# A hybrid encoder layer on one core: the last two and the first two input-projection tiles of adjacent blocks run in pairs

## The chip, the cores and the metric

The kernel runs on 1 core of one Trainium2 chip. The metric is device time in microseconds (us) of one execution. The time before is the median of three runs.

## What is computed

One layer, 2048 tokens, width 1024, all in float32:

```python
h = rms_norm(x, norm1_g)
p = h @ w_in                       # one projection, columns split among four mixers
o = concat([fox_attention(p_A), gated_delta(p_B), hgrn2(p_C), gla(p_D)])
x = x + o @ w_out
x = x + conv_glu_ffn(rms_norm(x, norm2_g))
```

The change is about `p = h @ w_in` alone: which of its column tiles run when.

## The kernel before

The tokens are cut into four blocks of 512. For each block `in_proj(b)` computes the projection in 23 tiles of 128 columns (`proj_fm`) and three of 256 (`proj_tm`). A float32 product is made of three matmuls on a high and a low part of each operand (`mm3`: L108 high by high, L109 high weights by low `h`, L110 low weights by high `h`), so that a 128-column tile over the eight row groups k of `h` takes 24 matmuls. Below, such a matmul with 512 columns of `h` is called a big one. `h` of a block lies in sixteen tiles `h_hi0..7` and `h_lo0..7`, one buffer each: `block_h(b)` loads each piece of x from HBM (L295, into a `w2` tile of a ring of five), multiplies it by the row scale on VectorE (L296), and writes `h_hi` on ScalarE (L300) and `h_lo` on VectorE (L301). So `h_hi[k]` of block b+1 can be written only after the last tile of block b has read `h_hi[k]`.

Weights come in halves of four k (`load_half`: a load into one of two `w_raw` tiles, L315, then a split into `w_hi`, L306 on ScalarE, and `w_lo`, L307 on VectorE, four buffers each). A tile's result lies in one of three PSUM banks `ps_mm` and leaves it through ScalarE; for a gate tile `put` runs a SiLU in five steps (L119 to L123, ScalarE and VectorE in turn), and stores the result to `p_scr` (L373). The SiLU's two buffers come from the same `w2` ring as x.

The tiles of a block come in this order: the gates' tile `FM_SMALL`, six tiles of the delta-rule mixer from `FM_GQ` on, HGRN2 and GLA tiles, and at last the gates of three mixers, between which the FoX tiles (`group_fox`, its last part the 256-column tile `TM_FV` with stores to `v_scr`, L893) are spread. The last three of a block before: `FM_LG, TM_FV, FM_LG + 1`; then block b+1 begins with `block_h`, `FM_SMALL` (`small_gates`, L412 on, a chain over ScalarE and VectorE that ends in a scan, L425, and eight transposes on TensorE, L436), and `FM_GQ`.

The projection is one stream of Python steps; the three linear mixers (`group_gdn`, `group_hg`, `group_gla`) are three others, and `weave` traces the step of whichever stream is due first: each step says how long it counts (`yield 0.25`). Work under `self.first()` gets a higher priority. The framework's scheduler then puts every engine's instructions into one fixed order, by these priorities and by when it reckons operands and buffers to be ready; each engine works its order off without overtaking, and so does SyncE's queue of DMAs. Small matmuls of the mixers (L647 to L670 the delta rule, L732 to L739 the attention pieces of HGRN2 and GLA) so stand between the big ones. After block 3's last tile the projection's pools close, and FoX attention loads its heads (L964).

Of the kernel before, what the change touches and what calls it, by code (L numbers as in the profile page):

```python
# [10 lines left out]
F32 = mybir.dt.float32  # L11
# [10 lines left out]
KT = D // 128  # L22
# [3 lines left out]
TB = 512  # L26
# [11 lines left out]
FM_SMALL, FM_FQ, FM_FK, FM_GQ, FM_GK, FM_GV, FM_GZ = 0, 1, 3, 5, 7, 9, 11  # L38
FM_HQ, FM_HF, FM_HG, FM_LQ, FM_LK, FM_LG = 13, 15, 17, 19, 20, 21
N_FM = 23  # L40
P_G, P_HF, P_HQ, P_LQ, P_LK, P_GATE, N_P = 0, 6, 8, 10, 11, 12, 18
# [37 lines left out]
class Kernel:  # L79
# [245 lines left out]
    def proj_fm(self, t):  # L325
# [5 lines left out]
                yield 0.25  # L331
        return ps

    def proj_tm(self, t, consume):
        mm = self.nc.tensor.matmul
        ps = [self.ps_mm.tile([128, 2, 256], F32, name="ps_mm") for _ in range(2)]
        for kk in range(4):
            hi, lo = self.load_half(self.i["w_tm"][t, kk])
            for tt in range(4):
                o = ps[tt // 2][:, tt % 2]  # L340
                ts = slice(tt * 128, (tt + 1) * 128)
                for k in (2 * kk, 2 * kk + 1):
                    s = slice(k % 2 * 256, k % 2 * 256 + 256)
                    mm(o, self.h_hi[k][:, ts], hi[:, s], start=(k == 0 and tt % 2 == 0), stop=False,  # L344
                       skip_group_check=True)
                    mm(o, self.h_hi[k][:, ts], lo[:, s], start=False, stop=False, skip_group_check=True)  # L346
                    mm(o, self.h_lo[k][:, ts], hi[:, s], start=False, stop=(k == KT - 1), skip_group_check=True)  # L347
                if tt % 2 and 2 * kk + tt // 2 < 6:
                    yield 0.125
        for tt in range(4):  # L350
            consume(tt, ps[tt // 2][:, tt % 2])

    def in_proj(self, b):
        nc = self.nc
        bs = slice(b * TB, (b + 1) * TB)
        with self.first():
            self.block_h(b, self.first_block() if b == 0 else None)
            for _ in self.small_gates(b):
                pass
        stats = self.block_stats(b + 1) if b < NB - 1 else iter(())  # L360
        def put(t, slot, scale=None, gate=None):
            next(stats, None)
            ps = yield from self.proj_fm(t)
            with self.first():
                o = self.w2()
                if gate is not None:
                    tmp = self.w2()
                    self.silu(o, ps, tmp, gate)
                elif scale is not None:
                    nc.scalar.activation(out=o, in_=ps, func=AF.Copy, scale=scale)  # L370
                else:
                    nc.scalar.copy(out=o, in_=ps)
                nc.sync.dma_start(out=self.p_scr[slot, :, bs], in_=o)  # L373
        def put_v(t, w):
# [3 lines left out]
                    nc.scalar.copy(out=o, in_=ps)  # L378
                    nc.sync.dma_start(out=self.lv_scr[w, b, :, tt], in_=o)
            yield from self.proj_tm(t, consume)  # L380
        yield
        for j in range(6):
            yield from put(FM_GQ + j, P_G + j)
            yield 0.25
        for j in range(2):
# [14 lines left out]
        for n, (t, c) in enumerate(((FM_GZ, C_GON), (FM_HG, C_HON), (FM_LG, C_LON))):  # L400
            for j in range(2):
                if n + j:
                    for size in fox:
                        yield size or 0.25
                        if not size:
                            break
                yield from put(t + j, P_GATE + 2 * n + j, gate=self.col(c))
                yield 0.25
        assert next(fox, self) is self


    def small_gates(self, b):  # L412
        nc = self.nc
        ps = yield from self.proj_fm(FM_SMALL)
        z = self.wg()
        nc.scalar.activation(out=z, in_=ps, func=AF.Identity, scale=self.col(C_SIGN), bias=self.sbias)
        nc.sync.dma_start(out=self.gk_scr[b], in_=z[0:16, :])
# [1 line left out]
        w = self.wg()  # L419
# [13 lines left out]
        for w, (t, r) in enumerate(((G, 96), (ls, 64))):  # L433
            ps = self.ps.tile([128, TB], F32, name="ps")
# [1206 lines left out]
```

## Time and profile before

| | us |
|---|---|
| median of three runs | 2995.86 (2993.44 to 3003.88) |
| the profiled execution | 2996.68 |
| its span, first to last instruction | 2994.9 |
| TensorE busy in the span | 2864.3 (96%) |
| VectorE busy | 2152.0 (72%) |
| ScalarE busy | 1596.3 (53%) |
| mean granted TensorE clock | 0.967 |

The page of a profile lists busy times, the chain of work that ended last and the costliest groups of instructions. The trace behind it answers finer questions: an engine's instructions in order of time, with the idle time before each and what ended it; busy time and granted clock by stretch. Times count from the span's first instruction. A clock of 1.00 is 2.4 GHz, of 0.50 is 1.2 GHz.

### The profile page before, as it was taken

How to read it: one execution, taken by the hardware profiler on the slowest of the kernel's cores; microseconds unless marked ns; L12 is line 12 of the kernel's file. 1: busy time of each engine (PE TensorE's matmuls, PEld its weight loads, DVE VectorE, ACT ScalarE, POOL GpSimd, SP SyncE). 2: the span in 40 equal slices, each digit the busy share in tenths (PEclk: the TensorE clock that was granted, in tenths of full speed). 3: DMA queues.
4: the chain of work that ended last, by engine and by line, in shares of the span. 5: the costliest groups of instructions: out<-in, count | busy, mean ns of one | idle time of the engine just before them, and what ended most of it. 6: DMA issues, size and time to landing. Idle time of an engine off the chain costs nothing.

```text
span 2994.9 us, 57398 instructions
## 1 busy us (share of the span) xinstructions
PE 2864.3 (96%) x21994; PEld 2335.9 (78%) x21994; DVE 2152.0 (72%) x4666; ACT 1596.3 (53%) x3171; POOL 127.5 (4%) x258
## 2 busy tenths in 40 slices
PE   7999999999999998999999999999999999999999
PEld 5777777787777777777788888878788888888787
DVE  6697778678767876667666655558777777886975
ACT  6575667566656665555666632343455544544443
POOL 0000010001000100000000000003000000000000
PEclk9999999799889997999999999999999999999999
DMA  5633463355235523876533322453222221847344
GB/s 179 183 100 126 139 181 100 112 165 166 80 104 171 165 66 103 222 205 203 137 107 103 102 67 66 141 184 116 85 84 75 85 85 60 281 142 242 130 136 145
DMA packets 268938, 400.08 MB, mean 134 GB/s; under 512 B 66612, under 2 KB 93124, under 8 KB 268152
## 3 DMA queue, kind: packets, MB, share of 16 engines
q1 hardware_dynamic: 268664, 396.43, 43.5%
q8 instruction: 172, 2.82, 0.4%
q14 instruction: 102, 0.84, 0.1%
HBM read 310.63 MB, written 85.70 MB: 132 GB/s over the span
## 4 chain that ended last, share of the span: by engine, by line
PE 73%; DVE 9%; DMA 9%; ACT 6%; issue 2%; SPq 0%; DVEq 0%; ACTq 0%
PE ps_mm L108 15%; PE ps_mm L109 15%; PE ps_mm L110 14%; PE pt L108 3%; PE pt L110 3%; PE pt L109 3%; DVE w_lo L307 2%; PE po L1033 2%; DMA w_raw<-w_fm 2%; PE pt L1019 2%; PE ps L732 1%; ACT w_hi L306 1%; PE ps_mm L344 1%; PE ps_mm L346 1%; PE ps_mm L347 1%
## 5 line engine op out<-in xcount | busy, mean ns | idle before, releaser
L307 DVE TENSOR_TENSOR w_lo<-w_raw,w_hi 128x512 fp32r<-128x512 f32 x386 | 268.8, 698 | 199.7 <-ACT w_hi L306 188.1
L306 ACT CAST w_hi<-w_raw 128x512 fp32r<-128x512 f32 x386 | 237.7, 617 | 281.2 <-PE ps_mm L109 179.4
L108 PE MATMUL ps_mm<-h_hi,w_hi 128*128 128x512 f32 x736 | 314.8, 429 | 15.7 <-ACT h_hi L300 7.7
L108 PE MATMUL ps_mm<-h,w_hi 128*128 128x512 f32 x768 | 308.2, 402 | 2.6 <-ACT h L1208 1.7
L109 PE MATMUL ps_mm<-h,w_hi 128*128 128x512 f32 x768 | 303.9, 396 | 0.0
L109 PE MATMUL ps_mm<-h_lo,w_hi 128*128 128x512 f32 x736 | 303.5, 413 | 0.0
L110 PE MATMUL ps_mm<-h,w_lo 128*128 128x512 f32 x768 | 303.4, 396 | 0.0
L110 PE MATMUL ps_mm<-h_hi,w_lo 128*128 128x512 f32 x736 | 302.1, 411 | 0.5 <-issue 0.4
L108 PE MATMUL ps_mm<-big,w_hi 128*128 128x512 f32 x456 | 183.6, 404 | 11.1 <-ACT big L306 6.7
L108 PEld LDWEIGHTS ps_mm<-h_hi,w_hi 128*128 128x128 f32 x736 | 144.3, 197 | 54.8 <-ACT h_hi L300 10.5
L110 PE MATMUL ps_mm<-big,w_lo 128*128 128x512 f32 x456 | 181.8, 399 | 0.0
L109 PE MATMUL ps_mm<-big,w_hi 128*128 128x512 f32 x456 | 181.7, 399 | 0.0
L110 PEld LDWEIGHTS ps_mm<-h,w_lo 128*128 128x128 f32 x768 | 144.4, 188 | 33.8
L108 PEld LDWEIGHTS ps_mm<-h,w_hi 128*128 128x128 f32 x768 | 144.1, 188 | 33.1 <-ACT h L1208 2.7
L110 PEld LDWEIGHTS ps_mm<-h_hi,w_lo 128*128 128x128 f32 x736 | 144.6, 196 | 31.0 <-DVE w_lo L307 1.5
L109 PEld LDWEIGHTS ps_mm<-h,w_hi 128*128 128x128 f32 x768 | 144.6, 188 | 30.9 <-DVE h L1209 1.4
L109 PEld LDWEIGHTS ps_mm<-h_lo,w_hi 128*128 128x128 f32 x736 | 144.6, 196 | 30.7 <-issue 3.2
L306 ACT CAST w_hi<-fo 128x512 fp32r<-128x512 f32 x135 | 79.5, 620 | 104.4 <-issue 36.8
L1238 DVE SCALAR_TENSOR_TENSOR y<-u,fconv,y 128x512 f32<-128x512 f32 x176 | 131.8, 749 | 3.8
L1382 DVE SCALAR_TENSOR_TENSOR y<-u,fconv,y 128x1024 f32<-128x1024 f32 x88 | 112.8, 1282 | 19.5 <-ACT y L1380 18.7
L307 DVE TENSOR_TENSOR p_lo<-pt,p_hi 128x512 fp32r<-128x512 f32 (+1 forms) x144 | 93.9, 657 | 37.9 <-ACT p_hi L306 37.8
L108 PE MATMUL pt<-w_hi 128*128 128x512 f32 x308 | 120.3, 391 | 0.0
(414 smaller groups left out, 7306.4 us busy)
## 6 DMA issues: line engine op xcount, KB each, us to landing
w_raw<-w_fm SPq DMA_DIRECT2D x184, 256.0 KB, 3.1
w_raw<-w_up SPq DMA_DIRECT2D x88, 256.0 KB, 2.6
fo<-w_down SPq DMA_DIRECT2D x88, 256.0 KB, 3.5
fo<-a_scr SPq DMA_DIRECT2D x88, 256.0 KB, 4.4
wr<-w_up SPq DMA_DIRECT2D x84, 256.0 KB, 2.7
p_scr<-w SPq DMA_DIRECT2D x72, 256.0 KB, 2.7
w_raw<-w_out SPq DMA_DIRECT2D x64, 256.0 KB, 3.7
w_raw<-w_tm SPq DMA_DIRECT2D x48, 256.0 KB, 3.0
```

The costliest lines, as they stand in the source:

```text
L108: mm(ps, w_hi, x_hi, start=start, stop=False, **k)
L109: mm(ps, w_hi, x_lo, start=False, stop=False, **k)
L110: mm(ps, w_lo, x_hi, start=False, stop=stop, **k)
L306: self.nc.scalar.copy(out=hi, in_=src)
L307: self.nc.vector.tensor_tensor(out=lo, in0=src, in1=f32(hi), op=ALU.subtract)
L344: mm(o, self.h_hi[k][:, ts], hi[:, s], start=(k == 0 and tt % 2 == 0), stop=False, skip_group_check=True)
L346: mm(o, self.h_hi[k][:, ts], lo[:, s], start=False, stop=False, skip_group_check=True)
L347: mm(o, self.h_lo[k][:, ts], hi[:, s], start=False, stop=(k == KT - 1), skip_group_check=True)
L1019: nc.tensor.transpose(pt[:, x * 128:x * 128 + 128], P[t][:, kt * 128:kt * 128 + 128], self.ident)
L1033: mm(po[:, c0:c0 + cn], vst[:, kt], part[:, kk * 256:kk * 256 + cn], start=(kt == 0 and part is hi), stop=(kt == nkt - 1 and part is lo), ...
L1238: nc.vector.scalar_tensor_tensor(out=y, in0=u[:, i:i + TB], scalar=w(i), in1=y, op0=ALU.mult, op1=ALU.add)
L1382: nc.vector.scalar_tensor_tensor(out=yt, in0=u[g][:, i:i + 2 * TB], scalar=f(i), in1=yt, op0=ALU.mult, op1=ALU.add)
```

## The change

`proj_pair` computes two tiles in step: for each k, six matmuls, three for either tile, and then a yield. `FM_SMALL` and `FM_GQ` are one pair, `FM_LG` and `FM_LG + 1` the other. The first pair is no longer under `first()` and traced at one go: it gives 0.25 of a step after each k, so that the mixers' steps are traced between. `TM_FV` now comes before both `FM_LG` tiles instead of between them. The two results of a pair are taken (`take`) after both are complete. `small_gates` gets its tile ready made.

```diff
+    def proj_pair(self, *ts):
+
+        out = [self.ps_mm.tile([128, TB], F32, name="ps_mm") for _ in ts]
+        for k in range(KT):
+            if k % 4 == 0:
+                w = [self.load_half(self.i["w_fm"][t][:, k // 4 * TB:(k // 4 + 1) * TB]) for t in ts]
+            s = slice(k % 4 * 128, k % 4 * 128 + 128)
+            for o, (hi, lo) in zip(out, w):
+                self.mm3(o, hi[:, s], lo[:, s], self.h_hi[k], self.h_lo[k], k == 0, k == KT - 1)
+            if k < KT - 1:
+                yield 0.25
+        return out
+
...
             self.block_h(b, self.first_block() if b == 0 else None)
-            for _ in self.small_gates(b):
-                pass
+        ps, gq = yield from self.proj_pair(FM_SMALL, FM_GQ)
+        with self.first():
+            self.small_gates(b, ps)
...
-        yield
-        for j in range(6):
+        take(gq, P_G)
+        yield 0.25
+        for j in range(1, 6):
...
-                yield from put(t + j, P_GATE + 2 * n + j, gate=self.col(c))
-                yield 0.25
+                if n < 2:
+                    yield from put(t + j, P_GATE + 2 * n + j, gate=self.col(c))
+                    yield 0.25
+        for j, ps in enumerate((yield from self.proj_pair(t, t + 1))):
+            take(ps, P_GATE + 4 + j, gate=self.col(c))
+        yield 0.25
```

The number of instructions on each engine stays as it was; their order changes, on TensorE from the first block to the start of the output projection, and not behind it. Lines below L334 stand 13 to 20 higher in the new kernel (L654 becomes L674).

On TensorE, the end of block 0 in the kernel before (`h_hi_240` and `h_hi_245` are k = 6 and 7, `h_lo_241` and `h_lo_246` their low parts; `ps_3477` a PSUM tile of a mixer):

```order
L108 MATMUL ps_mm<-h_hi_240,w_hi 128x512
L109 MATMUL ps_mm<-h_lo_241,w_hi 128x512
L110 MATMUL ps_mm<-h_hi_240,w_lo 128x512
L108 MATMUL ps_mm<-h_hi_245,w_hi 128x512
L109 MATMUL ps_mm<-h_lo_246,w_hi 128x512
L110 MATMUL ps_mm<-h_hi_245,w_lo 128x512
L782 MATMUL psl<-wl,l_kT 128x128 x2
L654 MATMUL ps<-g_R,w_2409 64x64 x4
L732 MATMUL ps_3477<-wl 32x32 x4
```

The same place now:

```order
L108 MATMUL ps_mm<-h_hi_245,w_hi 128x512
L109 MATMUL ps_mm<-h_lo_246,w_hi 128x512
L110 MATMUL ps_mm<-h_hi_245,w_lo 128x512
L108 MATMUL ps_mm<-h_hi_245,w_hi 128x512
L109 MATMUL ps_mm<-h_lo_246,w_hi 128x512
L110 MATMUL ps_mm<-h_hi_245,w_lo 128x512
L802 MATMUL psl<-wl,l_kT 128x128 x2
L674 MATMUL ps<-g_R,w_2409 64x64 x4
L752 MATMUL ps_3434<-wl 32x32 x4
L752 MATMUL ps_3434<-wx 32x32 x13
L682 MATMUL ps<-g_vn,w_1249 64x64 x4
```

Six big matmuls now use one k where three did, and from here to the first big matmul of block 1 stand 142 small matmuls (of the delta rule 8 `g_R`, 16 `g_vn`, 2 `gS`) where 124 stood (4, 4 and none).

The first big matmuls of block 1 before (`h_hi_3341` is k = 0, `h_hi_3348` k = 1, `h_hi_3355` k = 2):

```order
L108 MATMUL ps_mm<-h_hi_3341,w_hi 128x512 x2
L109 MATMUL ps_mm<-h_lo_3342,w_hi 128x512
L110 MATMUL ps_mm<-h_hi_3341,w_lo 128x512
L108 MATMUL ps_mm<-h_hi_3348,w_hi 128x512
L109 MATMUL ps_mm<-h_lo_3349,w_hi 128x512
L110 MATMUL ps_mm<-h_hi_3348,w_lo 128x512
L109 MATMUL ps_mm<-h_lo_3342,w_hi 128x512
L110 MATMUL ps_mm<-h_hi_3341,w_lo 128x512
```

and now:

```order
L108 MATMUL ps_mm<-h_hi_3341,w_hi 128x512 x2
L752 MATMUL ps_3645<-wl 32x32
L109 MATMUL ps_mm<-h_lo_3342,w_hi 128x512
L110 MATMUL ps_mm<-h_hi_3341,w_lo 128x512
L109 MATMUL ps_mm<-h_lo_3342,w_hi 128x512
L110 MATMUL ps_mm<-h_hi_3341,w_lo 128x512
L108 MATMUL ps_mm<-h_hi_3348,w_hi 128x512
L109 MATMUL ps_mm<-h_lo_3349,w_hi 128x512
```

Both tiles were already begun together; the second one's k = 0 now ends before k = 1 begins.

On SyncE's queue at the same boundary before (`w_raw<-x` belongs to the row scale of the block after; `w_raw<-w_fm` are weights; `w_3316` is the SiLU's result of `FM_LG + 1`):

```order
L252 DMA w_raw<-x 128x512
L315 DMA w_raw<-w_fm 128x512 x2
L295 DMA w_3338<-xT 128x512
L295 DMA w_3345<-xT 128x512
L373 DMA p_scr<-w_3316 128x512
L295 DMA w_3352<-xT 128x512
L295 DMA w_3359<-xT 128x512
```

and now (`w_3308` is the SiLU's result of `FM_LG`):

```order
L252 DMA w_raw<-x 128x512
L315 DMA w_raw<-w_fm 128x512
L389 DMA p_scr<-w_3308 128x512
L315 DMA w_raw<-w_fm 128x512
L295 DMA w_3338<-xT 128x512
L295 DMA w_3345<-xT 128x512
L389 DMA p_scr<-w_3316 128x512
L295 DMA w_3352<-xT 128x512
L295 DMA w_3359<-xT 128x512
```

The store of a SiLU's result now stands ahead of the first load of x.

## Rows read from the trace of the kernel before

**Rows 1.** The page, part 4: the chain that ended last, by engine.
```profile
PE 73%; DVE 9%; DMA 9%; ACT 6%; issue 2%; SPq 0%; DVEq 0%; ACTq 0%
```
**Rows 2.** Busy by stretch: length, PE, PEld, DVE, ACT, POOL, clock, DMA share, GB/s.
```profile
255.00:312.00 57.00, 51.02 (x885) 39.37 (x884) 39.36 (x117) 33.50 (x96) 0.00 (x0) 0.85 0.42 136
312.00:542.00 230.00, 220.66 (x2550) 181.64 (x2549) 175.60 (x495) 144.42 (x333) 9.87 (x7) 0.95 0.45 136
542.00:600.00 58.00, 53.28 (x892) 41.07 (x891) 40.57 (x121) 34.40 (x98) 0.00 (x0) 0.82 0.42 134
829.00:888.00 59.00, 52.74 (x878) 40.93 (x878) 39.17 (x116) 31.35 (x88) 0.00 (x0) 0.80 0.33 107
```
**Rows 3.** TensorE in time, block 0 to 1: start, duration, instruction, idle before.
```profile
262.70 0.39 PE L109 MATMUL ps_mm<-h_lo,w_hi 128*128 128x512 f32 x1
262.93 0.39 PE L110 MATMUL ps_mm<-h_hi,w_lo 128*128 128x512 f32 x1
...
263.69 0.68 PE L654 MATMUL ps<-g_R,w 64*64 64x64 f32 x8
...
269.44 0.47 PE L732 MATMUL ps<-wx 64*32 64x32 f32 x26 [2.10 <-issue]
...
272.97 1.22 PE L108 MATMUL ps_mm<-h_hi,w_hi 128*128 128x512 f32 x2 [1.59 <-ACT h_hi L300]
```
**Rows 4.** TensorE in time, block 2 to 3: the same two waits.
```profile
844.13 0.65 PE L732 MATMUL ps<-wx 64*32 64x32 f32 x32 [1.90 <-issue]
...
847.83 1.22 PE L108 MATMUL ps_mm<-h_hi,w_hi 128*128 128x512 f32 x2 [1.59 <-ACT h_hi L300]
```
**Rows 5.** VectorE in time, block 0 to 1.
```profile
266.70 0.75 DVE L123 SCALAR_TENSOR_TENSOR w<-ps_mm,cols,w 128x512 f32<-128x512 f32 x1
...
270.28 0.23 DVE L742 TENSOR_TENSOR l_acc<-ps,cst 128x64 f32<-128x64 f32 x1 [1.91 <-PE ps L739]
...
270.81 0.68 DVE L296 TENSOR_TENSOR w<-w,rr 128x512 f32<-128x512 f32 x1
```
**Rows 6.** ScalarE in time, block 0 to 1.
```profile
272.19 0.72 ACT L300 ACTIVATE h_hi<-w,cols 128x512 fp32r<-128x512 f32 x1
```
**Rows 7.** SyncE's DMA issues in time, block 0 to 1.
```profile
265.37 0.90 SPq L295 DMA_DIRECT2D w<-xT  x2
267.48 0.33 SPq L373 DMA_DIRECT2D p_scr<-w  x1
267.85 9.65 SPq L295 DMA_DIRECT2D w<-xT  x6
```
**Rows 8.** DMA issues: count, KB each, median us to landing.
```profile
p_scr<-w SPq DMA_DIRECT2D x72, 256.0 KB, 2.7
...
w<-xT SPq DMA_DIRECT2D x24, 256.0 KB, 3.4
```
**Rows 9.** The line that writes h_lo: duration ns min/median/max, first and last start.
```profile
L301 DVE SCALAR_TENSOR_TENSOR h_lo<-w,cols,h_hi x24: 743/746/753, 272.9 to 859.5; 128x512 fp32r<-128x512 f32 x24
```
**Rows 10.** DMA queues in 257 to 274 us: packets, MB, share.
```profile
q8 instruction: 3, 0.05, 1.2%
```
**Rows 11.** TensorE in time, around the gates' transposes of blocks 1 and 3.
```profile
297.47 0.45 PE L662 MATMUL ps<-g_vn,w 64*64 64x64 f32 x8 [1.30 <-DVE cols_tok L439]
...
872.88 1.14 PE L436 MATMUL ps<-ident,wg 128*128 128x128 f32 x8 [1.74 <-DVE wg L425]
```
**Rows 12.** Busy by stretch, columns as in rows 2: after block 1's first tiles.
```profile
269.60:276.50 6.90, 5.31 (x47) 4.05 (x40) 5.41 (x14) 4.42 (x12) 0.00 (x0) 0.51 0.60 195
...
294.00:300.40 6.40, 4.51 (x134) 3.24 (x132) 4.68 (x18) 1.83 (x6) 0.00 (x0) 1.00 0.50 159
300.40:310.60 10.20, 10.20 (x46) 7.73 (x43) 5.96 (x25) 6.31 (x23) 0.00 (x0) 0.50 0.23 79
```
**Rows 13.** After the last projection tile: SyncE's load and TensorE's first FoX matmul.
```profile
1131.13 1.08 SPq L964 DMA_DIRECT2D fa<-qk_scr  x2
...
1141.32 0.47 PE L990 MATMUL pt<-fa,qd 128*128 128x128 f32 x1
```

More of the change, by code (lines that the diff above doesn't have):

```diff
@@ L363, in put, with take @@
             ps = yield from self.proj_fm(t)
+            take(ps, slot, scale, gate)
+        def take(ps, slot, scale=None, gate=None):
             with self.first():
@@ L406, in in_proj, with small_gates @@
                             break
-                yield from put(t + j, P_GATE + 2 * n + j, gate=self.col(c))
-                yield 0.25
+                if n < 2:
[4 more added lines that the diff above has]
+        yield 0.25
         assert next(fox, self) is self
-    def small_gates(self, b):
+    def small_gates(self, b, ps):
         nc = self.nc
-        ps = yield from self.proj_fm(FM_SMALL)
         z = self.wg()
```

## The prediction

> **What bounds the kernel now.** I read the chain that ended last first: TensorE holds 73% of it [rows 1], so only time in which TensorE idles, or runs at its lower clock, can be given back. Then I read busy time by stretch, to see where that is. In the stretches around the block boundaries, 255 to 312, 542 to 600 and 829 to 888, TensorE is idle for 6.0, 4.7 and 6.3 us (length less PE busy) and the clock is 0.80 to 0.85; in the long stretch between two of them, 312 to 542, the clock is 0.95 [rows 2]. So 17 us of idle time, and the low clock beside it, are all that this change can reach.
>
> Then the boundary in time, block 0 to 1. Call T the start of block 0's last big matmul, 262.93. Block 1's first one starts at 272.97, T + 10.0. Between them TensorE works off small matmuls and idles twice: 2.10 us in the midst of a run of small matmuls, with nothing that it waited for ("issue"), and 1.59 us for `h_hi` [rows 3]. At block 2 to 3 the two waits are 1.90 and 1.59 [rows 4]; the boundary between shows the same pair. What makes `h_hi` late? x is asked for at T + 2.4 [rows 7] and takes 3.4 us to land [rows 8], so it is there at about T + 5.9. But its multiplication starts at 270.81, T + 7.9, since VectorE works in order and stood 1.91 us in front of L742, for small matmuls of TensorE [rows 5], those after the 2.10 us. `h_hi` starts at 272.19, T + 9.3 [rows 6]. The weak spot is not that `h_hi[0]` comes free too late. It comes free while the last tile still runs, and waits for its data.
>
> **The change, part by part.** The sum is made against the profiled execution's 2996.68 us (span 2994.9); that is 0.8 above the median of 2995.86, which I take off at the end. The count of instructions is the same on every engine, so nothing is removed; order moves.
>
> *The gap.* The pair ends both `FM_LG` tiles at once, so both SiLUs start at T. Before, the one SiLU's last step ended at 266.70 + 0.75, T + 4.5 [rows 5], and its store went at 267.48 [rows 7]. Now the first SiLU starts 0.7 earlier (three matmuls at 0.23, the distance of two starts in [rows 3]), so its store goes at T + 3.9. In SyncE's new order this store stands ahead of the first load of x, and behind it a weight load that waits for a `w_raw` tile. I put x at T + 5.3, 2.9 later than before, landed at T + 8.7 (3.4 more). The multiplication (0.68, [rows 5]) ends at T + 9.4 at best and `h_hi` (0.72, [rows 6]) at T + 10.1, with some delay behind mixer work T + 10.7 to 11.2. So the gap grows by 0.7 to 1.2 us. But it also holds more: 4 more of L654's kind (0.68 us for such a group of four, [rows 3]), 12 more `g_vn` and 2 `gS`, four and a half groups of about that size, 3.1 us; they overlap at their ends, so I count 2.5. Idle per boundary goes from 3.7 to 3.7 + 1.0 - 2.5 = 2.2: -1.5 each, -4.5 for three. Bounds: all of the idle goes (-10.5, three times the 3.5 to 3.7 of [rows 3, 4]), or the new groups wait on their own chain and fill nothing (+3.6).
>
> The 2.10 us are part of that. In 257 to 274 us the instruction queue moved three packets [rows 10]; the likeliest reading is that TensorE runs through a hundred small matmuls faster than instructions are fetched. The new gap has 142 small matmuls instead of 124, so I let this stall stay. The Trainium skill (Runtime: NRT & Kernel Launch, section Instruction fetch mechanics) calls the crossing of an instruction block mostly hidden. By that the stall would be something else and could go with the new order, some 5.5 us for three boundaries; the row, with nothing else to wait for, speaks for the fetch.
>
> *The first tiles of a block.* Both tiles already start together before (the order shows L108 twice on k = 0). What paces them is VectorE: 0.68 + 0.75 = 1.43 us for each k ([rows 5], [rows 9]), against 6 x 0.23 = 1.36 us of TensorE. A strict pair asks for them in just that rhythm, so pairing gains nothing here; before, the second tile lagged and filled the waits. The second SiLU's steps and four state updates now fall among them on VectorE, by estimate 2 us a boundary (0.75 for the last step, [rows 5], the rest short); TensorE has some fifty more small matmuls to put there. I take +1 each, +3 in all; bounds 0 (hidden) to +7.
>
> *The gates' chain.* After the first tile VectorE ends a scan, TensorE transposes, and TensorE's next instructions stand 1.30 us (block 1) and 1.74 us (block 3) for that chain [rows 11]. The same 66 big matmuls stand ahead of the transposes, but 165 small ones instead of 112, worth 1 to 2 us. I take -0.8 a boundary, -2.5 in all; bounds 0 to -3.9.
>
> *The bank and the move of `TM_FV`.* The pair takes two of the three banks, one of which `TM_FV` must leave first. Behind its last matmul stand over a hundred small ones before the pair, which cover that. Nothing, at most 0.8 at each of four places (the SiLU's last step holds a bank for 0.75, [rows 5]).
>
> *The end of block 3.* FoX's first loads wait for the SiLU's buffers, and go at 1131.13; its first matmul runs at 1141.32 [rows 13], with 10 us between. Two SiLUs end some 2 us later than one. Since TensorE has mixers to run I take +0.5, bounds 0 to 2.4.
>
> *The clock.* After the gap the clock is 0.51 for 6.9 us, and after the transposes, a stretch of 6.4 us with 4.5 busy, it is 0.50 for 10.2 us in which TensorE is full [rows 12]. The first stretch costs little, because VectorE paces it anyway. The second costs half its length, 5 us a boundary. The gap does not get shorter, so its stretch stays; the stretch at the transposes gets about a quarter less idle, and I take a tenth of the three times 5 us: -1.7.
>
> Sum: -4.5 + 3 - 2.5 + 0 + 0.5 - 1.7 = -5.2, that is 2996.7 - 5.2 - 0.8 = 2991 against the median.
>
> **The rivals.**
>
> *Idle time and clock come back together (faster).* The stall in the gap does not recur, the added groups fill it, and TensorE stays at its full clock after the transposes. For it: idle and low clock stand side by side in every boundary stretch [rows 2]. Against: the gap without big matmuls is no shorter. Price: -8 of the 10.5 us of gap idle, and half of 15 us of clock: -16, 2980. The Trainium skill (TensorE: Matmul & The Clock Gate, section HAM oscillation) has loops whose waits drop the clock again and again, and a rearranged loop that keeps it up; this trace shows the drop after each gap, and no run here yet shows a rearranged one.
>
> *x behind the stores (slower).* SyncE's queue works in order: the first x waits for the first SiLU's store, the third for its landing (2.7, [rows 8]), the fifth for the second SiLU's. Before, six loads took 9.65 us with such waits [rows 7]. If ScalarE, in order too, lets the second SiLU slip behind the mixers' copies, the second store moves from T + 7, where the five steps behind the first SiLU's would put it, to T + 10, and the later four k of the pair come 3 to 4 us late, with few small matmuls left. Price 4 us at three boundaries: 12 us, 3008. It decides when the second store goes later than about T + 9.
>
> *It does not do what it says.* The scheduler already overlaps the two first tiles, and `h_hi` is late for its data, not for its buffer; pairs then only shuffle. 0: 2996.
>
> **How the numbers follow.** A measurement of this kernel tells about 0.3%, 9 us, from no change; so faster means below 2987 and slower above 3005. My forecast, 2991, gets 0.42; the first rival 0.30, the second 0.17, the third 0.11. The forecast's own range, with the bounds of gap and first tiles, is 2983 to 3001. Faster: 0.27 from the first rival and 0.09 from the forecast's lower end, 0.36. Slower: 0.14 from the second rival, 0.02 from the forecast, 0.02 from the rest, 0.18. Same: 0.46. For eight in ten I leave out the far ends of both rivals: 2979 to 3004.
>
> **What would show it.** Right: at 263 to 285 the gap from the last to the first big matmul is 10 to 11.5 us with 1.5 to 3 us idle; the first x goes out 4 to 6 us after T, behind the store; the wait at the transposes is under 1 us; a stretch of half clock still follows each gap; the mean clock stays within 0.005 of 0.967. Wrong: a first x at T + 2.5 or before would make the gap term too small, a second store after T + 9 the second rival; a mean clock above 0.975 is the first rival; a change that arises after 1320 us, where the order of TensorE's instructions is as before, would be none of these.

## The result, and the profile after

| | before | after |
|---|---|---|
| median, runs side by side (us) | 2995.63 (2985.71 to 3003.88, 6 runs) | 3023.93 (3017.67 to 3030.98, 6 runs) |
| ratio, 95% interval | | 1.0092 (1.0071 to 1.0114) |
| the profiled execution, its span | 2996.68, 2994.9 | 3030.98, 3029.2 |
| mean granted clock of the profiled execution | 0.967 | 0.959 |

The changed kernel is 28 us slower. The forecast was 2991 with a range of 2979 to 3004; the time lies 20 us above that range.

The mean clock is the first thing to read. A run's span times its mean clock is the time that it would have taken at the full clock throughout, as far as TensorE sets the pace (called work below), and twice the span times (1 - clock) is the time that it spent at the lower level. The profiled run before gives 2994.9 x 0.967 = 2896 us of work and 198 us at half clock. Six runs after have spans of 3015.9 to 3029.2 and clocks of 0.958 to 0.963: on average 2903 us of work and 239 us at half clock. So of 28 us, half of 41, some 20 us, is the lower clock, and some 7 us is all the rest, idle time included. The side before is one run; 88 later runs of that kernel average 201 us at half clock, which bears out the 20 us, and 2887 us of work, which leaves the 7 us less sure.

Where it arises: I set the two traces side by side by the number of the projection's matmuls. The new kernel starts block 1 11.3 us late, block 2 16.7, block 3 28.0, ends the projection 22.6 late, and a further 12 come between 1146 and 1333 us. From there to the end, where TensorE's order is as before, the distance stays between 34 and 41.

The stretches of the new trace, in the columns of [rows 2] (start and end, length, then busy time and instructions of each engine, the granted clock PEclk, DMA share, GB/s):

```profile
core 0: us, PE busy (x) PEld busy (x) DVE busy (x) ACT busy (x) POOL busy (x), PEclk, DMA share, GB/s
239.00:246.20 7.20, 7.04 (x247) 6.27 (x246) 4.63 (x15) 4.52 (x10) 0.00 (x0) 0.91 0.36 117
246.20:255.00 8.80, 8.80 (x40) 6.62 (x40) 3.67 (x18) 2.99 (x12) 0.00 (x0) 0.50 0.00 0
264.00:321.00 57.00, 52.71 (x899) 41.68 (x887) 38.79 (x114) 33.63 (x93) 0.00 (x0) 0.79 0.41 126
...
275.60:289.30 13.70, 11.48 (x88) 8.67 (x88) 10.42 (x30) 6.54 (x18) 0.00 (x0) 0.50 0.69 223
...
309.70:319.90 10.20, 10.20 (x149) 8.17 (x137) 6.66 (x29) 3.69 (x14) 0.00 (x0) 0.50 0.27 86
```

The stretch of the boundary, 264 to 321, answers to 255 to 312 in [rows 2], where the clock was 0.85. It is now 0.79. But there is also half clock where there was none before, at 244.9 to 255.1, from just ahead of the last pair on, with TensorE busy for all of the 8.80 us from 246.2. The same places before:

```profile
239.00:246.20 7.20, 7.20 (x120) 6.61 (x118) 2.06 (x6) 4.33 (x9) 0.00 (x0) 1.00 0.13 39
...
244.00:255.00 11.00, 10.97 (x106) 9.85 (x106) 6.20 (x19) 5.47 (x15) 0.00 (x0) 1.00 0.29 96
```

That is the end of block 0. At the ends of blocks 1 and 2 the kernel before had half clock too, among `TM_FV`'s matmuls:

```profile
522.20:535.88 13.68, 13.68 (x122) 12.71 (x122) 3.30 (x10) 4.69 (x10) 0.00 (x0) 0.50 0.07 20
...
808.90:822.60 13.70, 13.70 (x122) 12.73 (x122) 3.32 (x10) 4.69 (x10) 0.00 (x0) 0.50 0.07 20
```

The new kernel has as much there (535.0 to 548.7 and 832.0 to 845.7), so nothing is added at these two. The new profile, the slowest of the six runs, has 52 us more of half clock than the one before: 10 of them at the end of block 0, 14 in the three gaps (6.8, 10.2 and 10.2 before, 13.7 each now), some 20 behind the projection (see e4), the rest spread over the blocks.

What did TensorE do before the clock fell? Its order of time after, from `TM_FV`'s last matmul to the pair's first (start, duration, line, tile, shape, count; a small float32 matmul counts as two records):

```profile
238.96 0.28 PE L360 MATMUL ps_mm<-w_hi,h_lo 128*128 128x256 f32 x1
...
239.26 0.51 PE L752 MATMUL ps<-wx 64*32 64x32 f32 x38
...
239.74 2.11 PE L645 MATMUL ps<-w,w 32*32 32x32 f32 x64
...
242.56 2.11 PE L654 MATMUL ps<-w,w 32*32 32x32 f32 x64 [0.16 <-ACT w L648]
244.59 1.00 PE L667 MATMUL ps<-gS,w 128*128 128x128 f32 x4
...
246.20 0.79 PE L108 MATMUL ps_mm<-h_hi,w_hi 128*128 128x512 f32 x1
246.79 0.63 PE L109 MATMUL ps_mm<-h_lo,w_hi 128*128 128x512 f32 x1
...
252.04 0.63 PE L108 MATMUL ps_mm<-h_hi,w_hi 128*128 128x512 f32 x1
252.47 0.63 PE L109 MATMUL ps_mm<-h_lo,w_hi 128*128 128x512 f32 x1
```

Between 239.2 and 246.2 there are 244 records of small matmuls (four of them 128x128), hardly any idle time, and not one matmul of the projection. Before, `TM_FV`'s 96 matmuls stood between these. The pair's first two matmuls then start 0.59 us apart and later ones 0.43, where at full clock such a start comes every 0.23 us [rows 3].

A long group alone is not enough, though. Ahead of the pair of block 3 stands one as long, with as many records, and the clock stays up:

```profile
1113.90:1120.60 6.70, 6.53 (x244) 6.02 (x242) 3.79 (x9) 1.71 (x5) 0.00 (x0) 1.00 0.32 116
1120.60:1134.00 13.40, 13.40 (x193) 10.74 (x192) 8.33 (x36) 7.32 (x21) 0.00 (x0) 1.00 0.01 1
```

It has two chains of 64 records of 64x64 (L627) where the groups of blocks 0 to 2 have two of 32x32 (L645, L654). The traces of e5 and e11 below hold four more such groups with 64x64 chains, and no half clock in them or in the 5 us behind; with 32x32 chains there are 13 more in e2 to e5 and e11, and in or behind each 6.8 to 13.7 us of half clock begin. So it also matters which small matmuls gather; no run here changes their size alone.

The gap between the blocks (T is 270.77), TensorE first:

```profile
270.77 0.39 PE L110 MATMUL ps_mm<-h_hi,w_lo 128*128 128x512 f32 x1
...
276.97 0.33 PE L752 MATMUL ps<-wx 64*32 64x32 f32 x6 [1.54 <-issue]
...
282.44 0.69 PE L682 MATMUL ps<-g_vn,w 64*64 64x64 f32 x8 [0.45 <-ACT g_vn L677]
...
284.30 1.22 PE L108 MATMUL ps_mm<-h_hi,w_hi 128*128 128x512 f32 x2 [0.31 <-ACT h_hi L300]
```

SyncE's queue in the same time, with the two SiLUs' stores and the first loads of x:

```profile
275.39 0.33 SPq L389 DMA_DIRECT2D p_scr<-w  x1
...
276.31 0.92 SPq L295 DMA_DIRECT2D w<-xT  x2
278.13 0.33 SPq L389 DMA_DIRECT2D p_scr<-w  x1
```

VectorE's first multiplication of x:

```profile
280.64 0.69 DVE L296 TENSOR_TENSOR w<-w,rr 128x512 f32<-128x512 f32 x1
```

And ScalarE, with its wait and the first `h_hi`:

```profile
282.02 0.36 ACT L677 COPY g_vn<-ps 64x256 f32<-64x256 f32 x1 [4.94 <-PE ps L674]
...
283.52 0.72 ACT L300 ACTIVATE h_hi<-w,cols 128x512 fp32r<-128x512 f32 x1
```

What ScalarE waited for at this place before:

```profile
270.94 1.00 ACT L753 COPY AT<-l_acc 32x64 f32<-32x64 f32 x4 [3.99 <-DVE l_acc L744]
```

The gap is 13.5 us long instead of 10.0 [rows 3], and TensorE idles for less of it than before: 2.3 us instead of 3.7. What grew is the time for its small matmuls: there are 142 instead of 124, and from 275.6 on they run at half clock, 8.7 us of the gap. At the other two boundaries the gap grows from 9.6 and 9.9 us to 13.6 and 15.2, with 2.4 and 3.9 us of idle time where 3.1 and 3.5 were.

### The profile page after: what moved, and what is told of

The parts are those of the page before. It is cut to its first block, busy times and chain, and to the rows that moved or that the text cites. A ratio compares the mean times of both kernels' runs of the same rounds, so it can differ in the third digit from the quotient of the medians.

```text
span 3029.2 us, 57361 instructions
## 1 busy us (share of the span) xinstructions
PE 2887.0 (95%) x21994; PEld 2353.3 (78%) x21994; DVE 2160.1 (71%) x4666; ACT 1596.2 (53%) x3171; POOL 127.5 (4%) x258
## 4 chain that ended last, share of the span: by engine, by line
PE 73%; DMA 9%; DVE 8%; ACT 7%; issue 2%; SPq 0%; DVEq 0%; ACTq 0%
PE ps_mm L108 15%; PE ps_mm L109 14%; PE ps_mm L110 14%; PE pt L108 4%; PE pt L110 4%; PE pt L109 4%; DVE w_lo L307 2%; PE po L1053 2%; PE ps L752 2%; PE pt L1039 1%; ACT w_hi L306 1%; DMA fo<-o_scr 1%; PE ps L627 1%; PE ps_mm L357 1%; PE ps_mm L359 1%
## 5 line engine op out<-in xcount | busy, mean ns | idle before, releaser
L307 DVE TENSOR_TENSOR w_lo<-w_raw,w_hi 128x512 fp32r<-128x512 f32 x386 | 276.6, 718 | 183.2 <-ACT w_hi L306 177.0
L108 PE MATMUL ps_mm<-h_hi,w_hi 128*128 128x512 f32 x736 | 316.2, 432 | 12.4 <-ACT h_hi L300 5.3
```

Of the source, the lines that this page charges most:

```text
L108: mm(ps, w_hi, x_hi, start=start, stop=False, **k)
L307: self.nc.vector.tensor_tensor(out=lo, in0=src, in1=f32(hi), op=ALU.subtract)
```

## The experiments

The theory after this reading: the loss is the clock, and the clock falls because small matmuls gather in long groups with no matmul of the projection between them. The rivals: the first pair does it; the pairing itself does it; x stands behind the stores and makes the gap longer. All ratios are to the kernel before, run beside the other on the same chip; clock, half-clock time and span x clock are means over the runs.

| kernel | median | ratio (95%) | clock | half clock | span x clock |
|---|---|---|---|---|---|
| before (88 runs beside e1 to e15) | 2988 to 2990 | 1 | 0.966 to 0.967 | 199 to 203 | 2885 to 2887 |
| the changed kernel (6 runs) | 3023.93 | 1.0092 (1.0071 to 1.0114) | 0.960 | 239 | 2903 |
| e1 first pair only | 2993.62 | 1.0012 (0.9987 to 1.0036) | 0.966 | 203 | 2889 |
| e2 last pair only | 3023.13 | 1.0117 (1.0070 to 1.0163) | 0.959 | 249 | 2897 |
| e3 move of `TM_FV` only | 3005.52 | 1.0059 (1.0035 to 1.0082) | 0.961 | 236 | 2887 |
| e4 last block as before | 3018.47 | 1.0106 (1.0067 to 1.0145) | 0.959 | 249 | 2892 |
| e5 after, x on another queue | 3017.79 | 1.0091 (1.0071 to 1.0111) | 0.959 | 246 | 2892 |
| e6 before, x on another queue | 2983.27 | 0.9987 (0.9968 to 1.0007) | 0.968 | 193 | 2887 |
| e7 pair, then `TM_FV` | 3011.29 | 1.0064 (1.0038 to 1.0090) | 0.960 | 242 | 2888 |
| e8 after, one filler | 3026.26 | 1.0122 (1.0087 to 1.0156) | 0.960 | 245 | 2902 |
| e9 before, one filler | 3024.98 | 1.0122 (1.0092 to 1.0151) | 0.961 | 236 | 2905 |
| e10 before, two fillers | 3015.74 | 1.0095 (1.0061 to 1.0128) | 0.969 | 187 | 2923 |
| e11 after, h early | 3001.57 | 1.0040 (1.0015 to 1.0064) | 0.968 | 189 | 2902 |
| e12 before, two h early | 2996.33 | 1.0022 (0.9997 to 1.0048) | 0.966 | 206 | 2890 |
| e13 before, four h early | 2999.68 | 1.0057 (1.0030 to 1.0084) | 0.964 | 218 | 2891 |
| e14 both pairs, `TM_FV` last, h early | 2988.00 | 0.9994 (0.9972 to 1.0017) | 0.969 | 188 | 2892 |
| e15 no pairs, `TM_FV` last, h early | 2980.37 | 0.9973 (0.9949 to 0.9997) | 0.971 | 171 | 2893 |

The kernel before itself shows how much hangs on the clock: in 88 runs of the one program, the four with a clock of 0.962 took a span of 2998 us on average, the four with 0.970 took 2975.5. These 22 us are close to the 24 that 0.008 of the span comes to, so that nearly all of the half-clock time counts at half its length.

### Which part of the change

**e1** leaves the end of a block as before, **e2** its beginning, **e3** moves `TM_FV` without any pair, **e4** keeps the changed kernel but for block 3's end:

```diff
 e1, from the changed kernel
-                if n < 2:
-                    yield from put(t + j, ...)
-                    yield 0.25
-        for j, ps in enumerate((yield from self.proj_pair(t, t + 1))):
-            take(ps, P_GATE + 4 + j, gate=self.col(c))
-        yield 0.25
+                yield from put(t + j, ...)
+                yield 0.25
 e2
-        ps, gq = yield from self.proj_pair(FM_SMALL, FM_GQ)
         with self.first():
+            ps = self.drain(self.proj_fm(FM_SMALL))
             self.small_gates(b, ps)
 e3, as e2, and
-        for j, ps in enumerate((yield from self.proj_pair(t, t + 1))):
-            take(ps, P_GATE + 4 + j, gate=self.col(c))
-        yield 0.25
+        for j in range(2):
+            yield from put(t + j, P_GATE + 4 + j, gate=self.col(c))
+            yield 0.25
 e4
-                if n < 2:
+                if n < 2 or b == NB - 1:
...
-        for j, ps in ...
+        if b < NB - 1:
+            for j, ps in ...
```

> Only the first pair of the change: FM_SMALL and FM_GQ run as a pair, traced step by step among the mixers; the end of each block is as before (FM_LG, TM_FV, FM_LG + 1). The change costs 28 us (3023.9 against 2995.6). Theory of the clock at the block's end: the harm is in the last pair, since TM_FV, moved ahead of both FM_LG tiles, leaves a stretch of small mixer matmuls of some 7 us before the pair (a new half-clock stretch at 244.9 to 255.1 in the changed kernel) and a longer gap behind it (13.5 us against 10.0). By it this kernel is within 6 us of the kernel before (2990 to 3002), with no half clock at 240 to 260 us. Rival, the first pair is the harm, because its matmuls no longer come at one go and the gates' chain ends later: 3012 to 3024, with most of the 52 us of added half clock (250.2 against 198.0) still there. If both add: about 3008.

> Only the last pair of the change: TM_FV ahead of FM_LG and FM_LG + 1 run as a pair; the block's beginning is as before (FM_SMALL at one go with its priority, then FM_GQ alone). Theory of the clock at the block's end: most of the 28 us, 3015 to 3027, with half clock before the pair and behind it. Rival, the first pair is the harm: 2990 to 3002. If both add: about 3010.

> Only the move of TM_FV ahead of FM_LG: no pairs at all, FM_LG and FM_LG + 1 run one after the other at the block's end, the beginning as before. It tells the order of the tiles from the pairing. If the move by itself bunches the mixers' small matmuls and drops the clock: 3012 to 3027. If the pairing is what matters (two SiLUs and two stores at once ahead of the first load of x, and big matmuls that end together): 2990 to 3002 here.

> The changed kernel, but in block 3 the end of the block is as before (FM_LG, TM_FV, FM_LG + 1, no pair). By aligned matmuls the two kernels drift apart by some 20 us up to the last big matmul of the projection and by another 12 us between 1170 and 1300 us, where the first FoX heads are loaded. If those 12 us come from block 3's end (two SiLUs at once, later buffers for FoX): 3012 here, with the drift over 1170 to 1300 gone. If they come from elsewhere, as a consequence of the boundaries before: 3020 to 3026.

e1 is the kernel before within its interval. e2 has the whole loss. So the first pair is neither a gain nor a harm, and the last pair with its move is everything. By their profiles e1 has 142 small matmuls in a gap of 11.9 to 12.4 us too; a longer gap alone is thus not the loss. e3, between its two expectations, parts the move from the pair: the move alone costs 0.6%, and its work is that of the kernel before (2887), so that its whole loss of 16 us is 34 us more of half clock. Its profile, of one of its faster runs (0.964), shows only a part of these 34 us. At the end of block 0 it has the new stretch ahead of `FM_LG`, without a pair:

```profile
239.00:246.00 7.00, 6.74 (x192) 6.12 (x188) 3.79 (x14) 3.98 (x9) 0.00 (x0) 0.79 0.36 118
246.00:256.50 10.50, 10.50 (x50) 7.56 (x48) 5.24 (x21) 3.33 (x13) 0.00 (x0) 0.50 0.00 0
```

By the medians the pairing adds about as much again, 7 us by the clock and 10 of work, though the two intervals touch. In e3 the gap between blocks 0 and 1 is 9.6 us long, in e2 13.3.

e4 fell between its two expectations and settles little. In the profiles the 12 us behind the projection go when block 3's pair goes. The kernel before, from its last projection matmul to the first matmul of the common end:

```profile
1123.50:1298.70 175.20, 157.61 (x1598) 131.36 (x1597) 112.32 (x337) 96.50 (x255) 0.17 (x1) 0.83 0.62 171
```

The same in the changed kernel:

```profile
1146.10:1333.20 187.10, 164.44 (x1598) 137.18 (x1597) 112.22 (x339) 98.20 (x257) 0.17 (x1) 0.79 0.60 167
```

And in e4:

```profile
1149.60:1325.20 175.60, 158.32 (x1599) 131.56 (x1598) 112.73 (x337) 96.77 (x255) 0.17 (x1) 0.83 0.62 172
```

187.1 falls to 175.6, with the clock back from 0.79 to 0.83. The timed runs do not show it: 1.0106 against 1.0092 for the changed kernel. Nor does the profile of e5 below, which keeps block 3's pair: from the last projection matmul to where the common order begins it takes 169.6 us, against 167.9 before, 166.6 in e4 and 179.9 in the changed kernel. Whether block 3's pair has a cost of its own stays open.

### Is it x behind the stores?

One line differs in **e5** (from the changed kernel) and **e6** (from the kernel before):

```diff
-                nc.sync.dma_start(out=xk, in_=self.i["xT"][k, ...])
+                nc.gpsimd.dma_start(out=xk, in_=self.i["xT"][k, ...])
```

> The changed kernel with one line different: block_h's loads of x are issued by GpSimd instead of SyncE, so that they no longer stand behind the first SiLU's store and weight loads in SyncE's queue (the first two loads have buffers long before; in the changed kernel they went at T + 5.5 and T + 7.7 only because of the queue, and the first big matmul came at T + 13.5 against T + 10.0 before). If the pair's own harm is x behind the store (rival 2 of the prediction): the first x goes before T + 2, the first big matmul comes at T + 9 to T + 10.5, and the three boundaries together give back 9 to 15 us: 3008 to 3015. If the gap is set by the mixers' small matmuls and by VectorE's and ScalarE's order, not by x: the gap stays at 12.5 us or more and the time at 3020 to 3028.

> The kernel before with the same one line: x loaded through GpSimd's queue. It takes the same delay out of the kernel before (first x at T + 2.4, first big matmul at T + 10.0, 1.59 us of wait for h_hi at each boundary). If x sets the gap there too: 1 to 2 us at each of three boundaries, 2987 to 2993. If VectorE's wait for small matmuls is what makes h_hi late: no change, 2993 to 2999.

In e5 the first x is asked for 25 us before the last big matmul (T is 269.1 there). Still the first big matmul of block 1 comes at T + 13.9, and the time is that of the changed kernel. GpSimd's queue in e5:

```profile
244.13 0.71 POOL L295 DMA_DIRECT2D w<-xT  x1 [36.67 <-DMA v_scr<-w]
```

VectorE's first multiplication of x in e5:

```profile
279.28 0.68 DVE L296 TENSOR_TENSOR w<-w,rr 128x512 f32<-128x512 f32 x1
```

And the wait of ScalarE in e5, ahead of its first `h_hi`:

```profile
280.53 0.37 ACT L677 COPY g_vn<-ps 64x256 f32<-64x256 f32 x1 [5.15 <-PE ps L674]
```

The first x has been there for some 30 us when VectorE comes to multiply it, since in its fixed order the multiplication stands behind the mixers' steps; and ScalarE stands 5.15 us in front of a copy for the delta rule, behind which `h_hi` is queued. So the first x behind the store does not set the gap. The loads after it still went late in e5, the second at 274.03, T + 4.9, once a buffer was free, so that e5 does not try them. In e6 the same edit gives nothing that can be told from the kernel before.

### Is it the move, or pairs wherever they stand?

**e7** has the pair ahead of `TM_FV`, which becomes the last tile; the pair's lines at the end go.

```diff
+                    if n == 2 and j:
+                        for i, ps in enumerate((yield from self.proj_pair(t, t + 1))):
+                            take(ps, P_GATE + 4 + i, gate=self.col(c))
+                        yield 0.25
                     for size in fox:
```

> The changed kernel with FM_LG and FM_LG + 1 still as a pair, but ahead of TM_FV, which is now the block's last tile. It tells the pairing from the move of TM_FV, from the other side than e3. If the move's harm is that the small matmuls of the mixers gather in two stretches of 7 to 8 us without a big matmul ahead of TM_FV and ahead of the pair (none such before), these go, the half clock of 245 to 255 goes, and with no SiLU at the end x is not held up: 2993 to 3005. If two big tiles computed in step are what costs, wherever they stand: 3010 to 3025. If TM_FV as the last tile makes a new wait (four stores and two banks at the end): above 3010 too, but with the longer wait behind TM_FV's last matmul.

It lies by its time in the second expectation, but not for the reason that I gave: its work is that of the kernel before (2888), no wait behind `TM_FV` makes it longer, and the loss is 40 us more of half clock. The stretches without a projection matmul are elsewhere now, 7.9 us at the boundary (272.0 to 279.9) and 8.6 ahead of the gates' transposes (303.1 to 311.8), where the kernel before had 6.4 (294.0 to 300.4).

### Full-width matmuls put between the small ones

**e8**, **e9** and **e10** add work whose result is not used, n = 1 (e8, e9) or 2 (e10) matmuls ahead of every group of 56 small ones:

```diff
                     p = self.ps2.tile([128, TB], F32, name="ps2")
+                    for _ in range(n):
+                        mm(p[:, 0:128], self.ident, self.cst[:, 0:128], start=True, stop=True)
```

> The changed kernel with one matmul more of 128x128 by 128 columns, result unused, ahead of every group of 56 small ones (32x32 and 32x64) of HGRN2's and GLA's attention pieces: 64 in all, at some 0.27 us (four 128x128 transposes take 1.09 us) at most 17 us of added work. It puts full-width matmuls into the stretches that have none, without moving anything else. Theory that the loss is TensorE's lower clock behind stretches of small matmuls: half-clock time falls from about 240 us to 180 or less, which gives back 30 us or more, so 3005 to 3012 in spite of the added work, with a clock above 0.967. Rival, that the clock has other reasons (idle, data) and the loss is the order of work: half clock stays at 230 to 260 and the time is 3030 to 3045.

> The kernel before with the same 64 matmuls more. By the clock theory its half-clock time of about 200 us falls too, to 150 or less, and pays for the added 17 us: 2980 to 2996. If the clock has other reasons: 3008 to 3016, with half clock at 195 to 215.

> The kernel before with two such matmuls ahead of every group, 128 in all, at most 35 us of added work. By the clock theory half clock falls further than with one (to 110 or less): 2980 to 3000. If the clock has other reasons: 3020 to 3035. It also gives the price of a filler by itself.

With one filler both expectations of my theory failed: half clock did not fall (245 and 236). In e9 it even rose by 33 us, and 20 us of work came on top. Part of that is that the scheduler also laid the small matmuls in another order, with new stretches such as 518.8 to 525.8, so that e9 is no clean test. With two, work grows by 38 us (0.30 us a filler, as in e9), and half clock is 187 instead of 203, far from the 110 that I had expected and within the spread of the runs (169 to 218 in e10's four, 185 to 216 in the seven before). In e10's profile most of it goes in the blocks 1 and 2, from 78 us to 20. These two blocks in the kernel before:

```profile
248.20:536.50 288.30, 272.95 (x3441) 222.03 (x3440) 216.67 (x617) 178.86 (x431) 9.87 (x7) 0.93 0.45 136
536.50:823.20 286.70, 270.95 (x3440) 220.48 (x3439) 215.94 (x616) 178.41 (x431) 9.70 (x7) 0.93 0.45 137
```

And in e10:

```profile
258.90:541.20 282.30, 269.70 (x3504) 222.61 (x3504) 219.97 (x616) 179.50 (x431) 12.30 (x7) 0.98 0.44 139
541.20:824.40 283.20, 269.39 (x3505) 222.32 (x3503) 219.88 (x616) 179.42 (x431) 12.31 (x7) 0.98 0.45 138
```

They are 6.0 and 3.5 us shorter in spite of the added matmuls. But e10 is no clean test either: its small matmuls also lie in another order, its long groups with hardly any idle time (513.5 to 521.1) have 64x64 chains, which the clock survived without fillers too, and TensorE idles 2 to 3 us less in each block. That the fillers keep the clock up fits all this, but is not shown; as a remedy they cost more than they give.

### What makes the gap

**e11** to **e13** change where the next block's h is traced: pieces k = 0 on are laid into the last tiles of the block (`EARLY` is 2 in e12, 4 in e11 and e13; e13 begins behind k = 2 instead of 3). `piece` is the body of the loop in `block_h`. VectorE's and ScalarE's order follows.

```diff
+    def early(self, b, k):
+        if b < NB - 1 and k >= 3 and k - 3 < EARLY:
+            with self.first():
+                if k == 3:
+                    self.nxt = [], []
+                self.piece(b + 1, k - 3, None, *self.nxt)
 in proj_pair (e11) or proj_fm of FM_LG + 1 (e12, e13), behind each k's matmuls
+            then(k)
 at the block's start
-            self.block_h(b, ...)
+                self.h_hi, self.h_lo = self.nxt
+                for k in range(len(self.h_hi), KT):
+                    self.piece(b, k, None, self.h_hi, self.h_lo)
```

> The changed kernel, but the pieces k = 0 to 3 of the next block's h (load of x, multiplication, h_hi, h_lo) are traced inside the last pair, behind its k = 3 to 6, instead of behind the whole pair. e5 showed that x was there 25 us ahead and the gap stayed at 13.9 us: VectorE's and ScalarE's fixed order has the multiplication and h_hi behind mixer steps that wait for TensorE's small matmuls. This run moves just that place. In TensorE's order the 142 small matmuls between the blocks become groups of at most 61. If the order of these two engines makes the gap, and the gap the half clock: no stretch without a big matmul longer than 5 us at the boundary, half clock down by 20 to 40 us, 3002 to 3010; the two stretches ahead of TM_FV and ahead of the pair stay and keep it above the kernel before. If the small matmuls only gather elsewhere: half clock at 235 to 250 and 3018 to 3026.

> The kernel before, with the pieces k = 0 and 1 of the next block's h traced inside its last tile (behind k = 3 and 4). By the same theory its boundary gaps of 10 us (half clock of 7 to 14 us behind each) shrink to 5 us or less: 2978 to 2986. If it does not matter: 2988 to 2996.

> The kernel before, with the pieces k = 0 to 3 of the next block's h traced inside its last tile (behind k = 2 to 5). In TensorE's order no group of over 60 small matmuls is left between the blocks, but the one ahead of the gates' transposes (125) stays. By the theory 2974 to 2984; if VectorE's extra work in the last tile holds up the weights or the SiLU: 2990 to 3000.

e11 bears the theory out for the changed kernel. Half clock falls to 189 us and the ratio from 1.0092 to 1.0040. Its stretches around the boundary:

```profile
239.00:248.00 9.00, 8.84 (x250) 8.05 (x248) 5.11 (x17) 4.68 (x10) 0.00 (x0) 0.72 0.60 194
248.00:258.00 10.00, 10.00 (x44) 7.42 (x44) 4.88 (x13) 2.18 (x4) 0.00 (x0) 0.57 0.04 14
258.00:300.00 42.00, 40.49 (x685) 31.28 (x684) 31.49 (x97) 28.59 (x78) 0.00 (x0) 1.00 0.30 97
300.00:312.00 12.00, 8.58 (x253) 6.72 (x251) 7.45 (x22) 5.42 (x17) 0.00 (x0) 0.83 0.51 157
```

There is no gap any more, the small matmuls stand between big ones, and the clock is 1.00 from 258 to 300. The stretch ahead of the pair is untouched and still pulls the clock down, as expected. What is left of the loss is work, 2902 us against 2887 in the kernel before beside it; where that lies I have not found out.

e12 and e13 missed. The boundary's gap goes there too, but the small matmuls gather at the next place, ahead of the gates' transposes, with half clock behind them. e12:

```profile
290.00:301.00 11.00, 8.27 (x247) 6.30 (x245) 7.18 (x21) 5.24 (x20) 0.00 (x0) 0.75 0.45 149
301.00:311.00 10.00, 10.00 (x43) 7.40 (x42) 4.43 (x20) 6.05 (x23) 0.00 (x0) 0.50 0.31 104
```

One gap closed is not yet a gain: the mixers' small matmuls must go somewhere.

### An order without long groups

**e14** is e7 with the next block's h traced inside `TM_FV`; **e15** is the same without any pair (`FM_SMALL` at one go, as in e2):

```diff
 in proj_tm, behind two token tiles of each kk
+                if tt % 2:
+                    then(2 * kk + tt // 2)
 in group_fox
-        yield from self.proj_tm(TM_FV, v_out)
+        yield from self.proj_tm(TM_FV, v_out, lambda k: self.early(b, k))
 e15, in place of the last pair
+                        for i in range(2):
+                            yield from put(t + i, P_GATE + 4 + i, gate=self.col(c))
+                            yield 0.25
```

> Both pairs of the change, but TM_FV behind the last pair (as in e7), and the next block's h pieces k = 0 to 3 traced inside TM_FV (as e11 does inside the pair). In TensorE's order no group of over 71 small matmuls stands at the end of a block or behind it, and the one ahead of the gates' transposes (125 to 128 in e7 and e13) is broken into groups of at most 60. By the clock theory half clock falls below the 200 us of the kernel before, to 150 to 185, with the work as before: 2970 to 2984, faster than both kernels. If the small matmuls' places are not what sets the clock: 2990 to 3012 as e7 and e13.

> The same without any pair: FM_LG, FM_LG + 1, TM_FV one after the other, FM_SMALL at one go as before, and the next block's h pieces 0 to 3 traced inside TM_FV. It tells whether pairs have a share at all in what e14 gives. By the clock theory the order of tiles and the place of h do it alone: half clock 160 to 190, 2972 to 2988, within 0.3% of e14. If the pairs help by themselves: 8 us or more above e14.

e14 came out slower than the theory said: 188 us of half clock, and the time of the kernel before. Against e7 it has 54 us less of half clock, but its work is 5 us more than that of the kernel before. e15 is the fastest of all, 0.9973 of the kernel before, and the only one whose interval lies below 1, if by little. It has 28 us less of half clock and 6 us more of work. The boundary in e15:

```profile
228.00:262.00 34.00, 33.79 (x542) 28.60 (x538) 24.35 (x68) 20.77 (x50) 0.00 (x0) 1.00 0.29 95
262.00:300.00 38.00, 35.69 (x730) 27.83 (x729) 28.20 (x86) 23.92 (x69) 0.00 (x0) 0.96 0.46 149
300.00:320.00 20.00, 19.88 (x154) 16.20 (x153) 13.39 (x36) 11.97 (x34) 0.00 (x0) 1.00 0.29 99
```

By the profiles the mean clock up to the projection's last matmul is 0.98 where it was 0.95, but from there to 1350 us 0.85 where it was 0.87: some of the small matmuls now gather behind the projection. So there is no sign that a pair helps, and e15, with the tiles one by one, is clearly ahead of the changed kernel, and of the kernel before by as little as these runs can tell.

## Why the prediction was wrong

**The bank and the move of `TM_FV`: the step that failed first.** I set it at nothing, because "over a hundred small ones" before the pair would cover the wait for a bank. No wait is there, so far I was right. But the cover is itself the harm: those matmuls, which stood among `TM_FV`'s before, are 7 us without one of the projection, and at the end of block 0 10.2 us at half clock follow where none were. e3 prices the move: 16 us, all of it lower clock. Where the rest of that arises is open, since at the ends of blocks 1 and 2 the kernel before has 13.7 us of half clock already.

**The clock: the term that was mis-sized.** I took -1.7 and measured +20 (198 to 239 us of half clock). I let the stretch behind the gap stay since "the gap does not get shorter", and called it cheap because VectorE sets the pace there. It began inside the gap, where TensorE sets the pace itself (before too: at 269.6, T + 6.7), and became 13.7 us long where 6.8, 10.2 and 10.2 were. Also, none of my cases had a clock that falls; the clock stood only on the side of gains. The mean over the six runs, 0.960, lies outside the 0.005 around 0.967 that I had named as the sign, though two of the six, 0.962 and 0.963, do not.

**The gap.** At the first boundary its idle time went as predicted, 3.7 to 2.3 where I had 2.2; over all three it fell by 1.7 us, not 4.5. Its length grew by 3.5, 4.0 and 5.2 us, where I had 0.7 to 1.2. The chain of x was right at its start: store at T + 4.6 (T + 3.9 predicted), first x at T + 5.5 (T + 5.3). From there it went wrong: multiplication at T + 9.9 instead of T + 8.7, `h_hi` done, and the first big matmul begun, at T + 13.5 instead of T + 10.1 to 11.2. And e5 shows that the first x was not what set it. The step that failed is the belief, in the first part, that `h_hi` waits for its data. I had seen VectorE stand in front of mixer work there, and still summed the new gap from x on, with up to 1.1 us for the mixers. `h_hi` waits for its turn on VectorE and ScalarE, behind copies for small matmuls, and e11, which moves that turn, closes the gap. The added groups of the delta rule, which I counted as filling, stand in just this chain: ScalarE's wait is now for one of them (4.94 us; 3.99 before, for another copy).

**The first tiles** were right: from the first to the 48th big matmul of blocks 1 to 3 it took 15.1, 16.1 and 16.0 us before and 16.6, 16.8 and 16.1 after, +0.8 on average where I had +1.

**The gates' chain** gave nothing where I had -2.5: the waits at the transposes, 1.30 and 1.74 [rows 11], are gone, but a wait of 1.62 for `g_vn` now stands just ahead of them, at 307.49, 600.90 and 898.26.

**The end of block 3**, +0.5, is a dozen us by the profile of the changed kernel, 2 by that of e5 with the same pair, and nothing by the timed runs of e4; open.

**The rivals.** The second, x behind the stores, had its number nearest (3008) and the wrong mechanism: the second store went at T + 7.4, below its own point of T + 9, and e5 shows that the first x does not set the gap; for the later ones the first tiles, +0.8, leave little. The first had the right quantity, the clock, with the wrong sign. The Trainium skill (TensorE: Matmul & The Clock Gate, section HAM oscillation), cited there, has the drop come from loops that wait for data. In this case the clock falls in a group of small matmuls with next to no wait: 7.04 us busy of 7.20.

**The 2.10 us "issue" idle** stayed in the changed kernel (1.54, 1.66 and 2.24 at the three boundaries), as I said; in e11, with big matmuls among the small, none of 0.8 us or more is left there. In e1, with the same 142 small matmuls in the gap, it is 0.75, 0.65 and 1.38. What makes it stays open.

## What to carry to other kernels

Before moving work on a busy TensorE, list what stands between its full-width matmuls before and after the move: a group of small ones that "covers" a wait can lower the clock for the big ones behind it, which costs more than the wait. Note their sizes too. Put the clock into the rivals on both sides, and split a measured difference into span x clock and half-clock time before looking for waits. When a result comes late although its operand is there, look at the order of the engine that makes it, and move the place where it is issued.

## What was not expected of the hardware

The granted clock fell with TensorE at 98% busy (7.04 of 7.20 us) on a group with two chains of 32x32 matmuls, and did not behind a group as long and as busy (6.53 of 6.70 us) with chains of 64x64. One program's mean clock varies from run to run, from 0.959 to 0.974 in 88 runs, and its span with it, from 3010 to 2967 us: a difference of 0.3% needs many runs, and the clock of each beside it.
